# Operand sums of a seven-product scheme made on VectorE behind plain units, and gate weights given the highest priority

## The chip, the cores and the metric

The kernel runs on one core of a Trainium2 chip. The metric is device time of one execution in microseconds (us). The engines have the profile's names: PE is TensorE, PEld its weight loads, ACT is ScalarE, DVE is VectorE, POOL is GpSimd, SP is SyncE, which issues the transfers.

## The reference

A diffusion backbone of two layers (DEPTH 2, D_MODEL 1024) over 256 context and 512 latent tokens, in fp32. Each layer has an adaLN-modulated RMSNorm, one input projection, three mixers (mLSTM, attention, gated DeltaNet), a gated sum and an output projection, and then the part of this case: a second norm and a gated MLP with a width-3 convolution over the tokens.

```python
def dwconv(u, w):
    ...
    up = jnp.pad(u, ((0, 0), (p, p), (0, 0)))
    out = up[:, 0:t] * w[0]
    for j in range(1, k):
        out = out + up[:, j:j + t] * w[j]
    return out
```

The MLP has D_FF = 2816 value and as many gate columns: each is a product of the normed tokens with `w_up`, a convolution, then value times silu(gate), then a product with `w_down`. The scans (mLSTM and DeltaNet) get their gates from 16 + 16 columns of `w_in`.

## The kernel before

Every fp32 product is made of three matmuls on operands split into a high part h (rounded to the type that PE takes, by ACT) and a low part l = x - h (by DVE): h.xh, h.xl and l.xh. The token operand of the MLP is `n01xh`, `n01xl` (tile names have the layer as their second character; 768 tokens in layer 0, 512 in layer 1).

`ffn` walks D_FF in groups f0 = 0, 4, .. 20 of four 128-column blocks, each as two pairs p0 = 0, 2. A pair is a gate unit (`f0g<f0><p0>`, 256 columns) and a value unit (`f0a<f0><p0>`). The down product of a group (`f0d0`, ...) comes between the gate and value units of the next. There are two kinds of unit. A plain unit (`gemm_fm`, and `gemm_first` for the first) has two blocks of 48 matmuls: 24 over 512 tokens, 24 over 256. A unit of seven products (`gemm7`) cuts columns, rows and tokens in halves and does seven products in place of eight: 84 matmuls over 384 tokens. It needs sums of weights (`s23`, `s4`; four 128x512 additions on POOL, L321, for each unit) and sums of the token operand, T1 to T4, each with a high part and a low part (`n01Th`, `n01Tl`; T2 overwrites a quarter of xh and xl). `norm_sums` makes those once, in layer 0 alone. In layer 0 before, pair 0 is plain, and the other ten pairs (20 units) use seven products. In layer 1 all units are plain.

Behind each block the conv takes the PSUM result: one ACT activation, and two DVE steps (511 or 255 wide) that read PSUM. In the value unit follow the product with the gate (POOL, in place on f0a), a cast (ACT, f0gh) and a subtraction (DVE, f0gl). Between the units PE does small blocks for later adaLN weights (`adp`, `adc`, fed by loads `ad`).

The Tile framework writes the order of each engine's instructions ahead of time, from a simulated timeline and from priorities; `self.high(n)` raises (or, if negative, lowers) the priority of what it encloses, and weight loads and splits have it raised by `self.prio`. On the chip each engine goes through its list in order. `gates_mm` loads the gate columns of `w_in` in three pieces (`g0raw`, `g1raw`), splits them (`g0w`, `g1w`) and multiplies.

Of the kernel before, what the change touches and what calls it, by code (L numbers as in the profile page):

```python
# [20 lines left out]
NT = SEQ + CTX  # L21
# [9 lines left out]
A_Q, A_K, A_V, A_O, A_G = 0, 256, 512, 1024, 1536  # L31
# [74 lines left out]
class Kernel:  # L106
# [201 lines left out]
    def gemm7(self, src, c0, x, nt, done, nm):  # L308
# [313 lines left out]
    def norm_sums(self):  # L622


        nc, N = self.nc, self.N
        nm, n = N["nm"], N["nt"] // 2
        xh, xl = N["x"]
        q = lambda v, k, t: v[:, 4 * k:4 * k + 4, n * t:n * t + n]
        R = {}
        for k, t in ((0, 0), (0, 1), (1, 1), (1, 0)):  # L630
            R[k, t] = self.q6(f"{nm}R{k}{t}").rearrange("p (k t) -> p k t", k=4)
            nc.gpsimd.tensor_tensor(out=R[k, t], in0=q(xh, k, t).bitcast(F32), in1=q(xl, k, t).bitcast(F32), op=ALU.add)

        def sub(o, a, b):
            nc.vector.tensor_tensor(out=R[o], in0=R[a], in1=R[b], op=ALU.subtract)
        sub((0, 0), (0, 1), (0, 0))
        sub((0, 1), (1, 1), (0, 1))
        sub((1, 1), (1, 1), (0, 0))
        sub((1, 0), (1, 0), (1, 1))
        T = {}  # L640
        for i, o in ((3, (1, 1)), (1, (0, 0)), (4, (1, 0)), (2, (0, 1))):
            if i == 2:
                T[i] = q(xh, 0, 1), q(xl, 0, 1)
            else:
                T[i] = [self.q6(f"{nm}T{v}{i}", F32R).rearrange("p (k t) -> p k t", k=4) for v in "hl"]
            self.split(*T[i], R[o])
        return xh, xl, T

    def norm_sq(self, j, a, b, eng=None):
        nc, N = self.nc, self.N  # L650
# [125 lines left out]
    def gates_mm(self, l, xs, gc):  # L776

        nc = self.nc
        nm = f"g{l}"
        W = self.I["w_in"][l]  # L780
        n = 288
        h, lo = [self.gw(f"{nm}w{u}", u).rearrange("p (k c) -> p k c", k=KD) for u in range(2)]
        for k0 in (0, 3, 6):
            nk = min(3, KD - k0)
            raw = self.T([128, 1024], f"{nm}raw{k0}", tag="wraw", bufs=4)[:, :nk * n].rearrange("p (k c) -> p k c", k=nk)
            rows = W[128 * k0:128 * (k0 + nk), :].rearrange("(k p) c -> p k c", p=128)
            for o, c0, m in ((0, A_G, 16), (16, C_G, 16), (32, B_Q + 512, 256)):
                nc.sync.dma_start(raw[:, :, o:o + m], rows[:, :, c0:c0 + m])
            self.split(h[:, k0:k0 + nk], lo[:, k0:k0 + nk], raw)
        self.bp = self.dr.tile([6, 128, 768], F32, name=f"bp{l}", tag=f"bp{l}")  # L790

        banks = ((self.pb, self.pb, self.pl), (self.pl, self.pc, self.pb)) if l else ((self.pl, self.pl, self.pc),) * 2
        for r in range(2):
            pss = [p(f"{nm}ps{r}_{i}")[:, 0:n] for i, p in enumerate(banks[r])]
            for i, ps in enumerate(pss):
                tt = 3 * r + i
                (a, _), xh, xl = xs[tt // 4]
                t = slice(128 * tt - a, 128 * tt - a + 128)
                for k in range(KD):
# [994 lines left out]
    def ffn(self, l, xs, nt):  # L1794
# [6 lines left out]
        for f0 in range(0, NFF, FG):  # L1801
            fn = min(FG, NFF - f0)
            gh, gl = [], []
            for p0 in range(0, fn, 2):
# [36 lines left out]
                if down and f0 + FG < NFF:  # L1841
                    self.gemm_fm(*down)
                    down = None
                if x7:
                    self.gemm7(U, 128 * (f0 + p0), x7, nt, done_a, f"{nm}a{f0}{p0}")
                else:
                    self.gemm_fm(U, 128 * (f0 + p0), 256, KD, xs, done_a, f"{nm}a{f0}{p0}")
                    if f0 + p0 == 0 and nt == NT:
                        x7 = self.norm_sums()
            segs = [((a, b), Blocks(gh, a, b), Blocks(gl, a, b)) for a, b in segb]  # L1850

            def done_d(j, res):
# [73 lines left out]
    def body(self):  # L1926
# [5 lines left out]
        for l in range(DEPTH):  # L1932
# [9 lines left out]
            with tc.tile_pool(name=f"t{l + 1}", bufs=1, reuse_waits="tile") as self.ph:  # L1942
# [95 lines left out]
```

## Time and profile before

| | |
|---|---|
| median of 3 runs | 2674.77 us (2668.91 to 2679.19) |
| profiled execution, its own time | 2679.46 us |
| span of its profile, mean granted clock of PE | 2677.7 us, 0.987 |
| busy: PE, PEld, DVE, ACT, POOL | 97%, 83%, 63%, 39%, 17% |

The busy shares are of the span. With PE at 97%, time can only come from stretches in which PE stands still or runs at a lower granted clock, or from fewer or shorter matmuls. The profile shows where those stretches are, and which engine PE waits for in each.

### The profile page before, as it was taken

Reading aid. Unit: us, or ns where it says so; the run is one execution under the profiler, and the core shown is the slowest. Engines: PE = TensorE matmul, PEld = TensorE weight load, DVE = VectorE, ACT = ScalarE, POOL = GpSimd, SP = SyncE. Lnnn points to the kernel's source line nnn. Section 1 sums busy time; section 2 is a strip of 40 time slices with the busy share of each in tenths; the row PEclk is TensorE's granted clock in tenths of the full one; section 3 lists DMA queues with packets and bytes.
Section 4 is the critical chain, followed back from the end, with each engine's and each line's share of the span. In section 5 each row is a group of like instructions: output and inputs, shape, how many; then the busy total and the mean of one; then the engine's idle time right before and its main releaser. Section 6 shows DMA issues by size and latency. Waiting matters only on the chain.

```text
span 2677.7 us, 44644 instructions
## 1 busy us (share of the span) xinstructions
PE 2584.4 (97%) x17161; PEld 2234.9 (83%) x17161; DVE 1699.3 (63%) x3605; ACT 1047.1 (39%) x2313; POOL 463.1 (17%) x362
## 2 busy tenths in 40 slices
PE   7999999999999997999999999999999999999999
PEld 5987988888888886899999988888877878888887
DVE  6666566746534658676786777856676646655555
ACT  5433355333432234343443454344633333433332
POOL 1010000001110426154445320000000203100000
PEclk9999999999999998999999999999999999999999
DMA  8364343546746322322212243522367675333332
GB/s 284 94 178 134 90 121 88 151 137 195 214 160 230 120 87 87 107 83 79 71 54 81 87 141 102 154 71 77 114 193 219 184 249 150 91 94 95 95 103 75
DMA packets 485223, 344.19 MB, mean 129 GB/s; under 512 B 48168, under 2 KB 450322, under 8 KB 484242
## 3 DMA queue, kind: packets, MB, share of 16 engines
q1 hardware_dynamic: 484721, 338.19, 42.6%
q8 instruction: 135, 2.21, 0.3%
q10 hardware_dynamic: 288, 3.15, 0.3%
q14 instruction: 79, 0.64, 0.1%
HBM read 285.23 MB, written 56.03 MB: 127 GB/s over the span
## 4 chain that ended last, share of the span: by engine, by line
PE 75%; DVE 10%; DMA 9%; issue 2%; ACT 1%; POOL 1%; SPq 1%; DVEq 0%; POOLq 0%; ACTq 0%
PE mg04p L265 1%; PE mg04p L266 1%; PE mg04p L264 1%; PE y0p L265 1%; PE y0p L264 1%; PE y0p L266 1%; PE adp L541 1%; PE mg14p L264 1%; PE mg14p L265 1%; PE mg14p L266 1%; PE y1p L264 1%; DMA m1mb<-g1rd 1%; PE y0op L264 1%; PE y0op L266 1%; PE y0op L265 1%
## 5 line engine op out<-in xcount | busy, mean ns | idle before, releaser
L1830 POOL TENSOR_TENSOR f1a<-f1a,f1g 128x512 f32<-128x512 f32 x22 | 28.5, 1295 | 311.8 <-DVE f1a L1815 292.3
L541 PE MATMUL adp<-ad,s 128*32 128x256 f32 x640 | 55.7, 405 | 6.5 <-DMA ad<-ada_w 5.6
L1830 POOL TENSOR_TENSOR f0a<-f0a,f0g 128x768 f32<-128x768 f32 x22 | 51.9, 2360 | 57.8 <-DVE f0a L1815 53.4
L1752 POOL TENSOR_TENSOR y0a<-y0a,y0g 128x768 f32<-128x768 f32 x16 | 33.2, 2079 | 118.1 <-DVE y0g L1749 115.8
L1107 POOL TENSOR_TENSOR m0qz<-m0qz,m0e 64x512 f32<-64x512 f32 x12 | 15.5, 1295 | 165.5 <-DVE mg04s5l L225 68.7
L541 PEld LDWEIGHTS adp<-ad,s 128*32 128x32 f32 x640 | 18.5, 112 | 26.3 <-issue 14.2
L1832 DVE TENSOR_TENSOR f0gl<-f0a,f0gh 128x768 fp32r<-128x768 f32 x22 | 31.0, 1411 | 8.5 <-ACT f0gh L1831 8.5
L1752 POOL TENSOR_TENSOR y1a<-y1a,y1g 128x512 f32<-128x512 f32 x16 | 24.2, 1513 | 57.8 <-DVE y1g L1749 56.6
L544 ACT COPY adr<-adp 128x256 f32<-128x256 f32 x40 | 14.8, 370 | 44.0 <-PE adp L541 42.8
L1831 ACT CAST f0gh<-f0a 128x768 fp32r<-128x768 f32 x22 | 18.4, 838 | 33.5 <-POOL f0a L1830 33.5
L1013 ACT ACTIVATE mg0t<-mg04p 128x512 f32<-128x512 f32 (+1 forms) x40 | 19.5, 486 | 25.2 <-PE mg04p L266 20.7
L1107 POOL TENSOR_TENSOR m1qz<-m1qz,m1e 64x512 f32<-64x512 f32 x8 | 11.2, 1406 | 102.9 <-DMA m1mb<-g1rd 45.7
L1821 ACT ACTIVATE f0g<-f0g 128x768 f32<-128x768 f32 x22 | 18.5, 846 | 22.8 <-DVE f0g L1815 22.8
L1749 DVE SCALAR_TENSOR_TENSOR y0g<-y0g,y0p 128x512 f32<-128x512 f32 (+1 forms) x32 | 17.3, 549 | 15.8 <-PE y0p L266 14.0
L1821 ACT ACTIVATE f1g<-f1g 128x512 f32<-128x512 f32 x22 | 13.9, 630 | 32.5 <-DVE f1g L1815 32.5
L1096 DVE SCALAR_TENSOR_TENSOR m0mb<-m0mb,g0a,cst 128x128 f32<-128x128 f32 x48 | 16.6, 404 | 15.3 <-DMA m0mb<-g0rd 14.3
L1773 DVE SCALAR_TENSOR_TENSOR hr<-y0op,y0gh,hr 128x512 f32<-128x512 f32 (+1 forms) x16 | 9.9, 617 | 25.8 <-PE y0op L266 25.8
L1169 POOL TENSOR_TENSOR rt<-rc,rw 128x256 f32<-128x256 f32 x4 | 3.0, 745 | 115.7 <-PE b0pk L1239 54.8
L1832 DVE TENSOR_TENSOR f1gl<-f1a,f1gh 128x512 fp32r<-128x512 f32 x22 | 15.1, 685 | 10.9 <-ACT f1gh L1831 10.7
L1831 ACT CAST f1gh<-f1a 128x512 fp32r<-128x512 f32 x22 | 13.5, 616 | 16.6 <-POOL f1a L1830 16.6
L1729 DVE TENSOR_TENSOR y0l<-y0ld,y0h 128x768 fp32r<-128x768 f32 x12 | 12.8, 1091 | 11.3 <-ACT y0h L1728 11.3
L1098 ACT ACTIVATE m0mb<-m0mb 128x512 f32<-128x512 f32 x12 | 7.6, 631 | 30.1 <-DVE m0mb L1096 25.4
(4586 smaller groups left out, 10220.2 us busy)
## 6 DMA issues: line engine op xcount, KB each, us to landing
ad<-ada_w SPq DMA_DIRECT2D x96, 512.0 KB, 4.3
mg04r<-w_in SPq DMA_DIRECT2D x20, 512.0 KB, 5.1
mg14r<-w_in SPq DMA_DIRECT2D x20, 512.0 KB, 6.0
y0g<-mg SPq DMA_DIRECT2D x24, 384.0 KB, 4.4
mg<-mg0t SPq DMA_DIRECT2D x24, 256.0 KB, 3.1
y0r<-w_branch SPq DMA_DIRECT2D x12, 512.0 KB, 3.6
mg<-mg1t SPq DMA_DIRECT2D x24, 256.0 KB, 3.5
y1r<-w_branch SPq DMA_DIRECT2D x12, 512.0 KB, 3.9
```

Source lines behind the costliest of these rows:

```text
L264: nc.tensor.matmul(o, hv[:, k, :], xh[:, k, :], start=(k == 0), stop=False)
L265: nc.tensor.matmul(o, hv[:, k, :], xl[:, k, :], start=False, stop=False)
L266: nc.tensor.matmul(o, lv[:, k, :], xh[:, k, :], start=False, stop=(k == nk - 1))
L541: nc.tensor.matmul(ps[32 * j:32 * j + 32, 0:256], self.s32[:, 2 * k:2 * k + 32], raw[:, j, :], start=(q == 0), stop=(q == 1), tile_positio ...
L1013: nc.scalar.activation(s, o, AF.Tanh, scale=0.5)
L1107: nc.gpsimd.tensor_tensor(out=qd[r, d], in0=qd[r, d], in1=e2[r], op=ALU.mult)
L1749: nc.vector.scalar_tensor_tensor(out=(a if i == BR[0] else gt)[:, s:e], in0=gt[:, s:e], scalar=1.0, in1=ps, op0=ALU.add, op1=ALU.mult)
L1752: nc.gpsimd.tensor_tensor(out=a[:, :nt], in0=a[:, :nt], in1=gt[:, :nt], op=ALU.add)
L1821: nc.scalar.activation(a[:, :nt], a[:, :nt], AF.Silu)
L1830: nc.gpsimd.tensor_tensor(out=a[:, :nt], in0=a[:, :nt], in1=keep[b][:, :nt], op=ALU.mult)
L1831: nc.scalar.copy(h, a[:, :nt])
L1832: nc.vector.tensor_tensor(out=gl[-1][:, b, :nt], in0=a[:, :nt], in1=h.bitcast(F32), op=ALU.subtract)
```

## The change

Pairs 0 and 2 of group 0 are plain now, and the seven products begin with pair 4, 18 units in place of 20. `norm_sums` is called ahead of the value unit of pair 2, at a priority lowered by 3000. It makes no sums on POOL: ten instructions of 128x1536 on DVE and four splits, in two buffers R in place of four. The split of T2, which overwrites xh and xl, is made by `last_sum()` behind the plain unit. The buffer s4 is single, and the pool of q6 tiles has 11 in place of 10. In `gates_mm` of both layers the loads and splits have their priority raised by 100000.

```diff
@@ -313,7 +313,7 @@
         xh, xl, T = x
         r0, r1 = [self.wraw(src[:, c0 + 128 * b:c0 + 128 * b + 128], KD, 128, f"{nm}r{b}") for b in range(2)]
         s23 = self.pi.tile([128, KD, 128], F32, name=f"{nm}s23", tag="s23", bufs=2)
-        s4 = self.pi.tile([128, 4, 128], F32, name=f"{nm}s4", tag="s4", bufs=2)
+        s4 = self.pi.tile([128, 4, 128], F32, name=f"{nm}s4", tag="s4", bufs=1)
         lo, hi = slice(0, 4), slice(4, 8)
 
         def half(out, a, b, op):
@@ -626,25 +626,37 @@
         nm, n = N["nm"], N["nt"] // 2
         xh, xl = N["x"]
         q = lambda v, k, t: v[:, 4 * k:4 * k + 4, n * t:n * t + n]
-        R = {}
-        for k, t in ((0, 0), (0, 1), (1, 1), (1, 0)):
-            R[k, t] = self.q6(f"{nm}R{k}{t}").rearrange("p (k t) -> p k t", k=4)
-            nc.gpsimd.tensor_tensor(out=R[k, t], in0=q(xh, k, t).bitcast(F32), in1=q(xl, k, t).bitcast(F32), op=ALU.add)
-
-        def sub(o, a, b):
-            nc.vector.tensor_tensor(out=R[o], in0=R[a], in1=R[b], op=ALU.subtract)
-        sub((0, 0), (0, 1), (0, 0))
-        sub((0, 1), (1, 1), (0, 1))
-        sub((1, 1), (1, 1), (0, 0))
-        sub((1, 0), (1, 0), (1, 1))
+        R = [self.q6(f"{nm}R{i}").rearrange("p (k t) -> p k t", k=4) for i in range(2)]
         T = {}
-        for i, o in ((3, (1, 1)), (1, (0, 0)), (4, (1, 0)), (2, (0, 1))):
-            if i == 2:
-                T[i] = q(xh, 0, 1), q(xl, 0, 1)
-            else:
-                T[i] = [self.q6(f"{nm}T{v}{i}", F32R).rearrange("p (k t) -> p k t", k=4) for v in "hl"]
-            self.split(*T[i], R[o])
-        return xh, xl, T
+
+        def op(o, a, b, op):
+            nc.vector.tensor_tensor(out=o, in0=a, in1=b, op=op)
+
+        def diff(i, j, k):
+
+            for o, v in zip(R, (xh, xl)):
+                op(o, q(v, *j).bitcast(F32), q(v, *k).bitcast(F32), ALU.subtract)
+            op(R[0], R[0], R[1], ALU.add)
+
+        def less(o, j, a):
+            op(o, q(xh, *j).bitcast(F32), a, ALU.subtract)
+            op(o, o, q(xl, *j).bitcast(F32), ALU.add)
+
+        def split(i, v):
+            T[i] = [self.q6(f"{nm}T{p}{i}", F32R).rearrange("p (k t) -> p k t", k=4) for p in "hl"]
+            self.split(*T[i], v)
+        diff(1, (0, 1), (0, 0))
+        split(1, R[0])
+        less(R[1], (1, 1), R[0])
+        split(3, R[1])
+        less(R[0], (1, 0), R[1])
+        split(4, R[0])
+        diff(2, (1, 1), (0, 1))
+        T[2] = q(xh, 0, 1), q(xl, 0, 1)
+
+        def last():
+            self.split(*T[2], R[0])
+        return (xh, xl, T), last
 
     def norm_sq(self, j, a, b, eng=None):
         nc, N = self.nc, self.N
@@ -784,9 +796,10 @@
             nk = min(3, KD - k0)
             raw = self.T([128, 1024], f"{nm}raw{k0}", tag="wraw", bufs=4)[:, :nk * n].rearrange("p (k c) -> p k c", k=nk)
             rows = W[128 * k0:128 * (k0 + nk), :].rearrange("(k p) c -> p k c", p=128)
-            for o, c0, m in ((0, A_G, 16), (16, C_G, 16), (32, B_Q + 512, 256)):
-                nc.sync.dma_start(raw[:, :, o:o + m], rows[:, :, c0:c0 + m])
-            self.split(h[:, k0:k0 + nk], lo[:, k0:k0 + nk], raw)
+            with self.high(100000):
+                for o, c0, m in ((0, A_G, 16), (16, C_G, 16), (32, B_Q + 512, 256)):
+                    nc.sync.dma_start(raw[:, :, o:o + m], rows[:, :, c0:c0 + m])
+                self.split(h[:, k0:k0 + nk], lo[:, k0:k0 + nk], raw)
         self.bp = self.dr.tile([6, 128, 768], F32, name=f"bp{l}", tag=f"bp{l}")
 
         banks = ((self.pb, self.pb, self.pl), (self.pl, self.pc, self.pb)) if l else ((self.pl, self.pl, self.pc),) * 2
@@ -1841,12 +1854,16 @@
                 if down and f0 + FG < NFF:
                     self.gemm_fm(*down)
                     down = None
+                if f0 + p0 == 2 and nt == NT:
+                    with self.high(-3000):
+                        sums, last_sum = self.norm_sums()
                 if x7:
                     self.gemm7(U, 128 * (f0 + p0), x7, nt, done_a, f"{nm}a{f0}{p0}")
                 else:
                     self.gemm_fm(U, 128 * (f0 + p0), 256, KD, xs, done_a, f"{nm}a{f0}{p0}")
-                    if f0 + p0 == 0 and nt == NT:
-                        x7 = self.norm_sums()
+                    if f0 + p0 == 2 and nt == NT:
+                        x7 = sums
+                        last_sum()
             segs = [((a, b), Blocks(gh, a, b), Blocks(gl, a, b)) for a, b in segb]
 
             def done_d(j, res):
@@ -1950,7 +1967,7 @@
                 else:
                     self.ada_fill(2)
                 self.spare = nt < NT
-                with self.inner(f"u{l}", 10):
+                with self.inner(f"u{l}", 11):
                     xs = self.ffn(l, xs, nt)
                 self.dump_h(f"hf{l}", nt)
                 if l + 1 < DEPTH:
```

DVE, behind the plain unit f0a00 of layer 0 (n01R, n01T are the sums, f0a and f0g conv steps, ada for later weights). Before:

```order
L635 TENSOR_TENSOR n01R_11192<-n01R_11194,n01R_11192 128x1536
L574 TENSOR_REDUCE ada_103<-adc_3_11517 128x4
L580 TENSOR_TENSOR ada_103<-ada_103,vec 128x16
L635 TENSOR_TENSOR n01R_11194<-n01R_11196,n01R_11194 128x1536
L574 TENSOR_REDUCE ada_103<-adc_4_11679 128x4
L635 TENSOR_TENSOR n01R_11196<-n01R_11196,n01R_11192 128x1536
L225 TENSOR_TENSOR n01xl<-n01R_11194,n01xh 128x4x384
L635 TENSOR_TENSOR n01R_11198<-n01R_11198,n01R_11196 128x1536
L225 TENSOR_TENSOR n01Tl_11205<-n01R_11196,n01Th_11204 128x1536
L1832 TENSOR_TENSOR f0gl_11107<-f0a_11182,f0gh_11106 128x768
L225 TENSOR_TENSOR n01Tl_11209<-n01R_11192,n01Th_11208 128x1536
```

After, at the same place; f0a02s0l is the low part of a plain weight:

```order
L633 TENSOR_TENSOR n01R_11339<-n01xh 128x1536
L633 TENSOR_TENSOR n01R_11340<-n01xl 128x1536
L1826 SCALAR_TENSOR_TENSOR f0a_11182<-f0a00p_0_11132,vec,f0a_11182 128x511
L225 TENSOR_TENSOR f0a02s0l<-f0a02r_11363,f0a02s0h 128x1024
L633 TENSOR_TENSOR n01R_11339<-n01R_11339,n01R_11340 128x1536
L1826 SCALAR_TENSOR_TENSOR f0a_11182<-f0a00p_512_11157,vec,f0a_11182 128x255
L1828 SCALAR_TENSOR_TENSOR f0a_11182<-f0a00p_0_11132,vec,f0a_11182 128x511
L633 TENSOR_TENSOR n01R_11340<-n01xh,n01R_11339 128x1536
L1828 SCALAR_TENSOR_TENSOR f0a_11182<-f0a00p_512_11157,vec,f0a_11182 128x255
L225 TENSOR_TENSOR n01Tl_11345<-n01R_11339,n01Th_11344 128x1536
L1826 SCALAR_TENSOR_TENSOR f0g_11248<-f0g02p_0_11198,vec,f0g_11248 128x511
L633 TENSOR_TENSOR n01R_11340<-n01R_11340,n01xl 128x1536
```

The sums stand between the conv steps and weight splits, ten additions or subtractions in place of four; the last split, of n01xl, comes 39 rows further on, here with its neighbours:

```order
L633 TENSOR_TENSOR n01R_11339<-n01xh 128x1536
L1828 SCALAR_TENSOR_TENSOR f0a_11419<-f0a02p_0_11369,vec,f0a_11419 128x511
L580 TENSOR_TENSOR ada_103<-ada_103,vec 128x16
L1828 SCALAR_TENSOR_TENSOR f0a_11419<-f0a02p_512_11394,vec,f0a_11419 128x255
L633 TENSOR_TENSOR n01R_11339<-n01R_11339,n01R_11340 128x1536
L1826 SCALAR_TENSOR_TENSOR f0a_11507<-f0a02p_0_11457,vec,f0a_11507 128x511
L1828 SCALAR_TENSOR_TENSOR f0a_11507<-f0a02p_0_11457,vec,f0a_11507 128x511
L225 TENSOR_TENSOR n01xl<-n01R_11339,n01xh 128x4x384
L1845 TENSOR_TENSOR f0gl_11427<-f0a_11419,f0gh_11426 128x768
L225 TENSOR_TENSOR f0g40w1l<-f0g40r_11521,f0g40w1h 128x1024
```

It is followed by the low part of the third weight of `f0g40`, the first unit of seven products now.

POOL at the same place (L1830, after L1843, is value times gate; L321 the weight sums; L632 the sums of the operand). Before:

```order
L1830 TENSOR_TENSOR f0a_11099<-f0a_11099,f0g_11027 128x768
L321 TENSOR_TENSOR f0g02s_11223<-f0g02r_11218,f0g02s_11222 128x512
L632 TENSOR_TENSOR n01R_11192<-n01xh,n01xl 128x1536
L632 TENSOR_TENSOR n01R_11194<-n01xh,n01xl 128x1536
L632 TENSOR_TENSOR n01R_11196<-n01xh,n01xl 128x1536
L632 TENSOR_TENSOR n01R_11198<-n01xh,n01xl 128x1536
L1830 TENSOR_TENSOR f0a_11182<-f0a_11182,f0g_11035 128x768
L321 TENSOR_TENSOR f0a02s_11381<-f0a02r_11377,f0a02r_11379 128x512
L225 TENSOR_TENSOR f0g02w4l<-f0g02s_11223,f0g02w4h 128x512
L321 TENSOR_TENSOR f0g40s_11547<-f0g40r_11543,f0g40r_11545 128x512
L321 TENSOR_TENSOR f0a02r_11379<-f0a02r_11379 128x512
```

After:

```order
L1843 TENSOR_TENSOR f0a_11099<-f0a_11099,f0g_11027 128x768
L1843 TENSOR_TENSOR f0a_11182<-f0a_11182,f0g_11035 128x768
L321 TENSOR_TENSOR f0g40s_11523<-f0g40r_11519,f0g40r_11521 128x512
L321 TENSOR_TENSOR f0g40r_11521<-f0g40r_11521 128x512
L321 TENSOR_TENSOR f0g40s_11523<-f0g40r_11521,f0g40r_11519 128x512
L321 TENSOR_TENSOR f0g40s_11524<-f0g40r_11519,f0g40s_11523 128x512
L1843 TENSOR_TENSOR f0a_11419<-f0a_11419,f0g_11248 128x768
L1843 TENSOR_TENSOR f0a_11507<-f0a_11507,f0g_11331 128x768
```

The four additions of 128x1536 and the weight sums of the units `f0g02` and `f0a02` are gone.

ACT at the start of layer 1 (g1w are the gate weights, c10k0a and c10k0t conv and silu of the first key block, c10qs1h a weight). Before:

```order
L1365 ACTIVATE c10k0a_16193<-c10kp_0_16045,vec 128x512
L224 CAST g1w_16267<-g1raw_16269 128x864
L224 CAST g1w_16267<-g1raw_16275 128x864
L224 CAST g1w_16267<-g1raw_16281 128x576
L1371 ACTIVATE c10k0t_16197<-c10k0a_16193 128x512
L224 CAST c10qs1h<-c10qr_16623 128x1024
L1365 ACTIVATE c10k0a_16200<-c10kp_1_16047,vec 128x256
```

After:

```order
L224 CAST g1w_16243<-g1raw_16245 128x864
L224 CAST g1w_16243<-g1raw_16251 128x864
L224 CAST g1w_16243<-g1raw_16257 128x576
L1378 ACTIVATE c10k0a_16169<-c10kp_0_16021,vec 128x512
L224 CAST c10qs1h<-c10qr_16599 128x1024
L1384 ACTIVATE c10k0t_16173<-c10k0a_16169 128x512
L1378 ACTIVATE c10k0a_16176<-c10kp_1_16023,vec 128x256
```

The three casts stand ahead of the conv step, and the weight cast c10qs1h ahead of the silu c10k0t.

## Rows read from the trace of the kernel before

**Rows 1.** The page, busy time of the engines

```profile
PE 2584.4 (97%) x17161; PEld 2234.9 (83%) x17161; DVE 1699.3 (63%) x3605; ACT 1047.1 (39%) x2313; POOL 463.1 (17%) x362
```

**Rows 2.** Window of the stretch, core 0, busy us of each engine

```profile
1034.15:1094.89 60.74, 42.47 (x225) 35.84 (x224) 50.42 (x41) 20.73 (x27) 42.72 (x15) 0.78 0.29 87
```

**Rows 3.** Waits of PE, 1015 to 1100 us: total, times, longest

```profile
PE adp L541 <- DMA ad<-ada_w: 5.6, 2, 5.4
...
PE f0g02x L334 <- ACT n01xh L224: 4.4, 1, 4.4
...
PE f0g02x L334 <- ACT n01Th L224: 2.6, 1, 2.6
```

**Rows 4.** Timeline of POOL: start, us, instruction

```profile
1029.32 1.85 POOL L1830 TENSOR_TENSOR f0a<-f0a,f0g 128x768 f32<-128x768 f32 x1
...
1033.37 16.88 POOL L632 TENSOR_TENSOR n01R<-n01xh,n01xl 128x1536 f32<-128x1536 f32 x4
...
1050.21 3.41 POOL L1830 TENSOR_TENSOR f0a<-f0a,f0g 128x768 f32<-128x768 f32 x1
...
1059.10 2.81 POOL L321 TENSOR_TENSOR f0g40s<-f0g40r,f0g40r 128x512 f32<-128x512 f32 x1
...
1074.29 1.27 POOL L321 TENSOR_TENSOR f0g40s<-f0g40r,f0g40s 128x512 f32<-128x512 f32 x1
```

**Rows 5.** Timeline of DVE: start, us, instruction

```profile
1021.78 1.21 DVE L225 TENSOR_TENSOR f0g02w0l<-f0g02r,f0g02w0h 128x1024 fp32r<-128x1024 f32 x1
...
1022.91 0.47 DVE L1813 SCALAR_TENSOR_TENSOR f0a<-f0a00p,vec,f0a 128x255 f32<-128x255 f32 x1
...
1034.92 0.75 DVE L1815 SCALAR_TENSOR_TENSOR f0a<-f0a00p,vec,f0a 128x511 f32<-128x511 f32 x1
...
1050.21 1.74 DVE L635 TENSOR_TENSOR n01R<-n01R,n01R 128x1536 f32<-128x1536 f32 x1
...
1051.98 3.25 DVE L635 TENSOR_TENSOR n01R<-n01R,n01R 128x1536 f32<-128x1536 f32 x1
...
1057.90 2.85 DVE L635 TENSOR_TENSOR n01R<-n01R,n01R 128x1536 f32<-128x1536 f32 x1
```

**Rows 6.** Timeline of PE: start, us, instruction

```profile
1034.15 0.34 PE L334 MATMUL f0g02x<-n01xh,f0g02w0h 128*128 128x384 f32 x1
...
1094.89 0.34 PE L334 MATMUL f0g40x<-n01xh,f0g40w0h 128*128 128x384 f32 x1
...
1131.59 0.39 PE L264 MATMUL f0d0p<-f0gh,f0d0s4h 128*128 128x512 f32 x1
...
1134.34 0.28 PE L264 MATMUL f0d0p<-f0gh,f0d0s4h 128*128 128x256 f32 x1
...
1135.75 0.38 PE L573 MATMUL adc<-cst,adr 128*128 128x128 f32 x2
...
1137.06 0.50 PE L264 MATMUL f0d0p<-f0gh,f0d0s5h 128*128 128x512 f32 x1
```

**Rows 7.** Window of one unit of seven products, its instructions alone

```profile
1175.00:1200.00 25.00, 15.07 (x84) 14.61 (x84) 2.75 (x5) 0.93 (x2) 1.00 0.11 32
```

**Rows 8.** The page, costliest groups: busy and mean ns

```profile
L1832 DVE TENSOR_TENSOR f0gl<-f0a,f0gh 128x768 fp32r<-128x768 f32 x22 | 31.0, 1411 | 8.5 <-ACT f0gh L1831 8.5
```

**Rows 9.** DMA issues of 1033 to 1060 us: KB, us to landing

```profile
f0g40r<-w_up SPq DMA_DIRECT2D x2, 512.0 KB, 5.2
```

**Rows 10.** Windows of 2 us behind the waits, all engines

```profile
1074.00:1076.00 2.00, 2.00 (x9) 1.99 (x8) 0.31 (x1) 0.00 (x0) 1.56 (x2) 0.54 0.26 61
...
1076.00:1078.00 2.00, 2.00 (x9) 2.00 (x8) 0.00 (x0) 0.00 (x0) 0.00 (x0) 0.60 0.61 200
```

**Rows 11.** Waits of PE, 1575 to 1600 us

```profile
PE g1ps L802 <- DVE g1w L225: 3.0, 1, 3.0
```

**Rows 12.** Timeline of ScalarE (ACT) at the start of layer 1

```profile
1578.00 2.29 ACT L224 CAST g1w<-g1raw 128x864 fp32r<-128x864 f32 x3
```

**Rows 13.** Waits of PE, 1100 to 1200 us

```profile
PE f0g42x L334 <- POOL f0g42w4l L225: 0.2, 1, 0.2
```

## Prediction

> **What bounds the kernel now.** I read the page first: TensorE (PE) is busy 97% of the span [rows 1], so only a stretch where it is not busy can give time back without removing products. The slices of the page show one such stretch behind the head, about 1,030 to 1,095 us. Its window [rows 2] shows PE busy for 42.47 of 60.74 us, at a mean granted clock of 0.78: it idles, and part of its work runs at the lower of its two levels. The waits of PE there [rows 3] name the cause: `f0g02x`, the first unit with seven products, waits for the operand sums `n01xh`, `n01Th` (only the largest rows are shown), and the ada weights and the next unit's split queue behind. The timeline of GpSimd (POOL) [rows 4] has the four additions that begin the sums: 16.88 us, from 1033.37 to 1050.2, begun just when the plain unit `f0a00` ends. VectorE (DVE) then subtracts and splits beside POOL's weight sums; there a 128x1536 subtraction takes 2.85 us (beside `f0g40s`) or 3.25 us (beside the f0a multiply), alone 1.74 us [rows 5].
>
> **What the change costs and moves.** The place is the time from the start of `f0g02` at 1034.15 to the start of `f0g40` at 1094.89, 60.74 us [rows 6].
>
> Plain units in place of two of seven products. From the down products of group 0 [rows 6]: twelve 512-column matmuls take 1134.34 - 1131.59 = 2.75 us, twelve of 256 columns 1135.75 - 1134.34 = 1.41 us. A plain unit has 48 of each: 4 x 4.16 = 16.64 us. A unit of seven products is 84 matmuls, 15.07 us busy [rows 7]. So the two units cost 2 x 1.57 = 3.1 us more work. One ada block (16 + 2 small matmuls) is 1137.06 - 1135.75 = 1.31 us [rows 6].
>
> The new stretch without waits: 1034.15 + 2 x 16.64 + 2 x 1.31 = 1070.0 is where `f0g40` could start, 24.9 us sooner. The order has one more ada block behind that point than before, so 1.3 us goes back: **23.6 us** at most from this place.
>
> What VectorE must do meanwhile. POOL gives up the four additions, and the weight sums of two units (no row of them stands in the order after). The f0a multiply that came at 1029.32 [rows 4] no longer has three weight sums ahead, so I let the sums start at 1031.7 on DVE. From there to the end of `n01xl` the order of the changed kernel has, on DVE: 14 of 128x1536 (10 sums, 4 splits) at 1.74 = 24.4; ten 511-wide conv steps at 0.75 = 7.5; eight 255-wide at 0.47 = 3.8; four weight splits at 1.21 = 4.8; one f0gl at 1.41; 0.5 for tiny ones: 42.4 us [rows 5, 8]. Uncontended, T2's low part is ready at 1074.1. `f0g40` needs it after 12 + 12 matmuls (4.3 us, at a seventh of 15.07 us for 12), an ada block, and a few matmuls on T2's high part (0.5 us, my estimate): about 1070.0 + 4.3 + 1.3 + 0.5 = 1076.1. So DVE has 2.0 us to spare; the conv steps that release PSUM banks between the sums have margins of the same size.
>
> What takes the margin. POOL still does one f0a multiply and the four weight sums of `f0g40` beside that chain (its second raw tile is issued once `f0a02s1l` has been read, about 1052.8 by the same walk, and lands some 5.2 us later [rows 9]). By the pairs in [rows 4, 5] the multiply costs DVE 3.25 - 1.74 = 1.51 us, each weight sum 2.85 - 1.74 = 1.11: 5.95 us together. DVE is late by 5.95 - 2.0 = 4.0 us, and PE waits that long at the start of `f0g40`, in one or several pieces. After the waits near 1071 to 1074 the clock was 0.54 and 0.60 over 4 us [rows 10], which gave away 2 x 0.46 + 2 x 0.40 = 1.7 us; I take it once. Residual: 5.7 us. Bounds: 0 (all hidden), and 14 x 1.11 - 2.0 = 13.5 us with 3.4 of clock, 16.9 us, if POOL met every one of the 14. I stay with 5.7, as POOL's list there has five instructions.
>
> The Trainium skill (SBUF — State Buffer, "SBUF: two separate sides") says that a VectorE instruction with two SBUF operands and a GpSimd instruction exclude one another for the whole instruction. Its sum would be POOL's own times, 1.85 + 4 x 1.27 = 6.9 us in place of 5.95, so 1 us less gain; the rows lie near it (1.74 + 1.27 = 3.01 against 2.85 and 2.81), and the sum goes by the rows.
>
> Gate weights first. In layer 1 PE waits 3.0 us for `g1w` [rows 11]. The order after moves only the three casts on ScalarE, 2.29 us [rows 12], ahead of `c10k0a`; on DVE the low parts still stand behind the conv steps, which now start later by up to 2.3 us, partly taken up by the wait for `c10qs1h`. I reckon 1 us lost there. In layer 0 the same three casts move ahead of `c00k0a`, and `c00k0t` is no longer behind them: some 0.7 us gained. The g0raw loads pass ad_3_3 and ad_1_0 to ad_1_2 on SP's queue, six issues earlier; the PE work on these waits for earlier adaLN work anyway. Net 0, bounds -3 and +3 (the wait gone, or doubled).
>
> One s4 buffer in place of two. The fourth weight sum of a unit now stands behind the w4 split of the unit before on POOL. PE waits for a w4 split only 0.2 us in such a place [rows 13]. Cover: the unit is 15 us long and the sum 1.27. I take 0; without cover it costs 1.27 us for each of 18 calls, 23 us. The order of layer 1's mixers also shifts (some 480 rows of PE, the same instructions): 0, bounds -3 and +3.
>
> **Sum.** 23.6 - 5.7 = 17.9 us off the profiled execution's 2679.46: 2661.6. That execution is 4.7 us above the median of 2674.77, so the predicted median is **2657**. A measurement here can tell about 0.5%, 13.4 us, from no change.
>
> **Rivals.** (A) The forecast, partly hidden: 2657, chance 0.48, own range 2650 to 2662. (B) All hidden: POOL's five instructions fall beside conv steps that read PSUM, which were not stretched (0.75 us at 1034.92, during POOL's additions [rows 4, 5]). Then 23.6: **2651**, chance 0.17. Against it: the DVE list has no gap to fall into. (C) DVE much later: the upper bound of 16.9 us, 2674.8 - 6.7 = **2668**; PE then waits at each PSUM bank and at T3, T2 and T1 in turn. For it: any idle time of DVE in its list, a cast on ScalarE that comes late, counts in full once the 2.0 us are gone; and 24.4 of its 42.4 us are open to contention. Chance 0.27. (D) Nothing to see, 2671 to 2678: the conv steps of `f0g02` and `f0a02` queue behind sums, and the stall of before only moves; it would need 20 us of new waits. Chance 0.04. (E) Slower: the single s4 buffer. If POOL, in its order, holds the f0a multiply behind a fourth sum that waits for the w4 split of a unit not yet reached by PE, every seven-product unit shows a wait. The price must pass 17.9 + 13.4 = 31.3 us, 1.7 us for each of 18 calls, against 1.27 us for the sum alone; at 2.5 us each the time is 2657 + 45 = **2702**. Against it: those units wait 0.2 us now. Chance 0.04.
>
> The skill's rule, read as a result of its own, gives 2658 and falls in (A).
>
> **How the numbers follow.** Leaving 1 in 10 on either side: below, (B) and a better split of layer 1, 2648; above, the larger part of (C), 2669. Faster by over 0.5% means below 2661.4: most of (A), all of (B) and a little of (C), 0.66. Slower: 0.04. Same: 0.30.
>
> **What would show it.** Right: POOL has no 128x1536 additions; `f0g40` begins near 1070 to 1076; the window from 1034 has PE above 0.9 busy and the clock near 1; PE's remaining wait there names `n01xh`, `n01xl` or `f0g40w23l`, 3 to 6 us in all; the wait for `g1w` is still about 3 to 4 us. Wrong: waits of PE for conv steps inside `f0g02` or `f0a02`, a 128x1536 instruction of DVE above 2.2 us on average, new waits for w4 splits in units 4 to 20, or more than 3 us lost in the mixers of layer 1.

## The result and the profile after

The changed kernel takes 2659.69 us (median of 5 runs, 2656.56 to 2661.14) against 2674.77 us: ratio 0.9934, 95% interval 0.9919 to 0.9948. Timed again beside other kernels (e9 below) the ratio was 0.9914, 0.9901 to 0.9928, so 18 to 23 us are gained by the ratios, which are not the quotients of the medians but lie within 0.001 of them; the two medians themselves differ by 15.1 us. Forecast were 17.9 us, and a median of 2657 where 2659.69 came.

The page of the kernel after, busy times; it answers to [rows 1]:

```profile
PE 2586.3 (97%) x17185; PEld 2235.7 (84%) x17185; DVE 1689.9 (64%) x3599; ACT 1042.6 (39%) x2305; POOL 420.8 (16%) x348
```

The stretch from the start of `f0g02` (1040.86 now; the window is cut at 1040.90) to the start of `f0g40` (1078.20), by the windows of the changed kernel (span, then busy us of PE, PEld, DVE, ACT and POOL, granted clock, DMA share, GB/s), and all of PE's waits from 1035 to 1095; they answer to [rows 2, 3, 6]:

```profile
1040.90:1078.20 37.30, 36.71 (x230) 30.70 (x229) 36.16 (x37) 15.34 (x20) 12.46 (x5) 1.00 0.32 97
```

```profile
PE f0g40x L334 <- DVE ada L580: 0.6, 1, 0.6
```

60.74 us have become 37.30, PE is busy for 36.71 of them, and the clock stays at 1.00. A single wait of 0.6 us is left. The stall is not shortened: it is gone, 23.4 us.

DVE and POOL of the kernel after in that stretch (start, us, instruction); they answer to [rows 4, 5]:

```profile
1040.89 1.75 DVE L633 TENSOR_TENSOR n01R<-n01xh 128x1536 f32<-128x1536 f32 x1
...
1053.13 2.74 DVE L633 TENSOR_TENSOR n01R<-n01R,n01xl 128x1536 f32<-128x1536 f32 x1
...
1066.51 2.45 DVE L633 TENSOR_TENSOR n01R<-n01xl 128x1536 f32<-128x1536 f32 x1
...
1069.54 2.18 DVE L225 TENSOR_TENSOR n01Tl<-n01R,n01Th 128x1536 fp32r<-128x1536 f32 x1
...
1074.00 1.34 DVE L225 TENSOR_TENSOR f0g40w23l<-f0g40s,f0g40w23h 128x1024 fp32r<-128x1024 f32 x1 [1.14 <-ACT f0g40w23h L224]
...
1081.80 1.76 DVE L225 TENSOR_TENSOR n01xl<-n01R,n01xh 128x1536 fp32r<-128x1536 f32 x1 [0.15 <-ACT n01xh L224]
```

```profile
1033.84 1.84 POOL L1843 TENSOR_TENSOR f0a<-f0a,f0g 128x768 f32<-128x768 f32 x1 [29.84 <-DVE f0a L1828]
1051.03 3.23 POOL L1843 TENSOR_TENSOR f0a<-f0a,f0g 128x768 f32<-128x768 f32 x1 [15.35 <-DVE f0a L1828]
1064.80 2.55 POOL L321 TENSOR_TENSOR f0g40s<-f0g40r,f0g40r 128x512 f32<-128x512 f32 x1 [10.54 <-DMA f0g40r<-w_up]
1067.43 2.68 POOL L321 TENSOR_TENSOR f0g40r<-f0g40r 128x512 f32<-128x512 f32 x1
1070.18 2.70 POOL L321 TENSOR_TENSOR f0g40s<-f0g40r,f0g40r 128x512 f32<-128x512 f32 x1
1072.96 1.30 POOL L321 TENSOR_TENSOR f0g40s<-f0g40r,f0g40s 128x512 f32<-128x512 f32 x1
1078.68 3.24 POOL L1843 TENSOR_TENSOR f0a<-f0a,f0g 128x768 f32<-128x768 f32 x1 [4.42 <-DVE f0a L1828]
```

DVE's list runs from 1040.89 to 1081.80 + 1.76 = 1083.56, 42.7 us. Where POOL works beside it, the instruction of POOL is stretched (2.55 to 2.70 for a weight sum that takes 1.30 at 1072.96, 3.23 and 3.24 for a multiply that takes 1.84 at 1033.84), by 6.8 us in all. Of DVE's sums and splits only three are (2.74, 2.45, 2.18, against 1.74 or 1.75), by 2.1 us. PE at the start of `f0g40`:

```profile
1078.20 0.42 PE L334 MATMUL f0g40x<-n01xh,f0g40w0h 128*128 128x384 f32 x1 [0.60 <-DVE ada L580]
...
1082.45 0.38 PE L573 MATMUL adc<-cst,adr 128*128 128x128 f32 x2
...
1083.68 1.06 PE L541 MATMUL adp<-ad,s 128*32 128x256 f32 x14
...
1084.96 0.34 PE L334 MATMUL f0g40x<-n01xl,f0g40w23h 128*128 128x384 f32 x1
```

`n01xl`, the last split, is ready at 1083.56, and the first matmul that reads it starts at 1084.96: 1.4 us are to spare.

### The profile page after: what moved, and what is told of

Its sections match the earlier page's. It is cut to its first block, busy times and chain, and to the rows that moved or that the text cites. A ratio compares the mean times of both kernels' runs of the same rounds, so it can differ in the third digit from the quotient of the medians.

```text
span 2657.9 us, 44659 instructions
## 1 busy us (share of the span) xinstructions
PE 2586.3 (97%) x17185; PEld 2235.7 (84%) x17185; DVE 1689.9 (64%) x3599; ACT 1042.6 (39%) x2305; POOL 420.8 (16%) x348
## 3 DMA queue, kind: packets, MB, share of 16 engines
q1 hardware_dynamic: 484721, 338.19, 42.7%
## 4 chain that ended last, share of the span: by engine, by line
PE 80%; DVE 8%; DMA 6%; issue 2%; ACT 1%; SPq 1%; POOL 1%; DVEq 0%; ACTq 0%; POOLq 0%
PE mg04p L265 2%; PE mg04p L266 2%; PE mg04p L264 2%; PE adp L541 1%; PE y0p L264 1%; PE y0p L265 1%; PE y0p L266 1%; PE mg14p L264 1%; PE mg14p L266 1%; PE mg14p L265 1%; PE y1p L264 1%; PE y1p L265 1%; PE y1p L266 1%; DMA ad<-ada_w 1%; PE y0op L265 1%
## 5 line engine op out<-in xcount | busy, mean ns | idle before, releaser
L1843 POOL TENSOR_TENSOR f1a<-f1a,f1g 128x512 f32<-128x512 f32 x22 | 28.5, 1295 | 312.1 <-DVE f1a L1828 292.6
L1843 POOL TENSOR_TENSOR f0a<-f0a,f0g 128x768 f32<-128x768 f32 x22 | 52.5, 2389 | 95.6 <-DVE f0a L1828 95.6
L1120 POOL TENSOR_TENSOR m0qz<-m0qz,m0e 64x512 f32<-64x512 f32 x12 | 16.6, 1383 | 166.5 <-DVE b0a3P L1338 69.4
L1845 DVE TENSOR_TENSOR f1gl<-f1a,f1gh 128x512 fp32r<-128x512 f32 x22 | 15.1, 685 | 10.9 <-ACT f1gh L1844 10.7
L1844 ACT CAST f1gh<-f1a 128x512 fp32r<-128x512 f32 x22 | 13.5, 616 | 16.6 <-POOL f1a L1843 16.6
```

Of the source, the lines that this page charges most:

```text
L1120: nc.gpsimd.tensor_tensor(out=qd[r, d], in0=qd[r, d], in1=e2[r], op=ALU.mult)
L1843: nc.gpsimd.tensor_tensor(out=a[:, :nt], in0=a[:, :nt], in1=keep[b][:, :nt], op=ALU.mult)
L1844: nc.scalar.copy(h, a[:, :nt])
L1845: nc.vector.tensor_tensor(out=gl[-1][:, b, :nt], in0=a[:, :nt], in1=h.bitcast(F32), op=ALU.subtract)
```

## The experiments

Theory 1: the gain is made in that stretch, because plain products hide the sums. Rival: it is the engine (GpSimd's additions) that counted. For the rest of the span the question is which of the smaller differences between the two profiles belong to the change, and which to the execution. Each kernel's ratio is to the kernel before, on the same chip (before: 2679.6 us for e1 to e4, 2679.43 for e5 to e8, 2680.83 for e9 to e12).

**e1, the raised priority alone.** The kernel before with

```diff
-            for o, c0, m in ((0, A_G, 16), (16, C_G, 16), (32, B_Q + 512, 256)):
+            with self.high(100000):
+                for o, c0, m in ((0, A_G, 16), (16, C_G, 16), (32, B_Q + 512, 256)):
...
```

> The kernel before with the raised priority of the gate weights alone; sums, units and s4 as before. Theory 1 (all of the gain is in the stretch from f0g02 to f0g40): the time is that of before, ratio 0.999 to 1.001; the 3.0 us wait for g1w in layer 1 becomes a wait of about 3.3 us for c10kq, and the 6 us by which layer 1's mixers are shorter in the profile after do not show again, since they are run-to-run variation. Rival theory (the changed order of layer 1's mixers, which comes with the gate priority, is worth 6 us and the changed head costs 3): 2671 to 2672 us, the mixers of layer 1 shorter by 5 to 7 us and the head longer by about 3 in its profile.

2675.79 us, ratio 0.9986 (0.9976 to 0.9995), faster by 0.14%, 3.8 us. The interval reaches theory 1's 0.999 to 1.001 as well as the rival's figure (as a ratio 0.9986 to 0.999), so the time alone does not decide. The profile speaks for the rival: layer 1's mixers took 663.3 us for 673.8, and the head was 3 us longer. The wait in layer 1 moved as expected (c10kq 2.9, g1w 0.7).

**e2, the change without the raised priority.**

```diff
-            with self.high(100000):
-                for o, c0, m in ((0, A_G, 16), (16, C_G, 16), (32, B_Q + 512, 256)):
...
+            for o, c0, m in ((0, A_G, 16), (16, C_G, 16), (32, B_Q + 512, 256)):
```

> The changed kernel without the raised priority of the gate weights. Theory 1: the whole gain stands here, 2657 to 2662 us, f0g40 begins 44 us after f0a00 ends (60.7 before) and PE waits under 1 us in between. Rival theory (the mixers of layer 1 gain by the gate priority): 3 us slower than the changed kernel, 2662 to 2665 us, and the mixers of layer 1 as long as before.

2666.07 us, 0.9951 (0.9939 to 0.9963), 13.1 us less than before by the ratio. The stretch takes 37.6 us and PE waits 0.9 us in it, so the mechanism there is theory 1's. (The 44 us expected are a difference between two traces, 1078.20 - 1034.15; the kernel after has 37.3.) Whether the whole gain stands here the time leaves open: as ratios, theory 1 gave 0.9934 to 0.9952 and the rival 0.9952 to 0.9964. The profile speaks for the rival, as the mixers of layer 1 took 681.3 us.

**e3, one s4 buffer alone.** The kernel before with

```diff
-        s4 = self.pi.tile([128, 4, 128], F32, name=f"{nm}s4", tag="s4", bufs=2)
+        s4 = self.pi.tile([128, 4, 128], F32, name=f"{nm}s4", tag="s4", bufs=1)
```

> The kernel before with one s4 buffer in place of two; only the order of GpSimd changes. In the profile after, the time from f0g40 to f0g200 is 2.1 us longer than before, and f0a162 waits 2.2 us for its w4 split. Theory 1 (the single buffer costs this): 2676 to 2677 us, the same wait at f0a162x, the time from f0g40 to f0g200 longer by 1.5 to 2.5 us. Rival (variation of the run, or the sums' new place): no wait for a w4 split above 0.5 us, 2674 to 2675 us.

2681.89 us, 1.0014 (1.0004 to 1.0024), slower by 0.14%, 3.8 us (2.3 us by the medians). Its profile has the wait of the kernel after; PE's waits of e3, 1440 to 1500 us:

```profile
PE f0a162x L334 <- POOL f0a162w4l L225: 2.1, 1, 2.1
```

f0a162 to f0g200 takes 18.1 us in place of 16.6; from f0g40 to f0g200 it is only 0.7 us more, less than expected. POOL and SP of the kernel after show the way there:

```profile
1446.59 2.01 POOL L321 TENSOR_TENSOR f0a162s<-f0a162r,f0a162s 128x512 f32<-128x512 f32 x1
1454.82 1.30 POOL L321 TENSOR_TENSOR f0a200s<-f0a200r,f0a200r 128x512 f32<-128x512 f32 x1 [6.22 <-DMA f0a200r<-w_up]
...
1457.45 2.25 POOL L225 TENSOR_TENSOR f0a162w4l<-f0a162s,f0a162w4h 128x512 fp32r<-128x512 f32 x1
...
1448.63 1.45 SPq L233 DMA_DIRECT2D f0a200r<-w_up  x2
```

f0a162's fourth weight sum now comes late in POOL's list (1446.59) and ends at 1448.60. It reads a raw weight tile, and SP issues the next unit's load, f0a200r, at 1448.63, 0.03 us later. Those data land at 1454.8; POOL's list has two sums of f0a200 ahead of f0a162's w4 split, for which PE waits 2.2 us.

**e4, sums on VectorE with one plain pair.**

```diff
-                if f0 + p0 == 2 and nt == NT:
+                if f0 + p0 == 0 and nt == NT:
...
-                    if f0 + p0 == 2 and nt == NT:
+                    if f0 + p0 == 0 and nt == NT:
```

> The changed kernel with one plain pair in place of two: the sums are all made on VectorE, but beside f0a00, and seven products begin with f0g02 as before. Theory 1 (the cover by 36 us of plain products is what hides the sums; VectorE alone needs 44 us for its list): PE still waits some 20 us at f0g02, 2664 to 2672 us. Rival theory (taking GpSimd's 17 us out is what counts, wherever the sums stand): under 2661 us, since two units fewer are plain, and under 8 us of waits at f0g02 and f0a02.

2682.2 us, 1.0003 (0.9991 to 1.0015): nothing gained, slower than both theories had it (as ratios 0.996 to 0.999, and under 0.9949). PE's waits of e4, 990 to 1095 us:

```profile
PE f0g02x L334 <- ACT n01xh L224: 9.8, 1, 9.8
PE adp L541 <- DMA ad<-ada_w: 2.0, 1, 2.0
...
PE f0g02x L334 <- DVE n01xl L225: 1.9, 1, 1.9
```

The stretch from f0g02 to f0g40 takes 54.3 us, 6.4 less than before. The waits of f0g02 in it are 13.4 us, where theory 1 had some 20 and the rival under 8. The stretch ahead of it (f0g00 to f0g02) takes 43.7 for 40.9, the head is 1.8 us longer, f0a162 1.6 and layer 1's mixers 3.8, so nothing is left. Without the second plain pair most of the stall stays, though VectorE makes the sums: the rival falls.

**e5, sums as before at the new place.** Four additions on GpSimd, four subtractions and four splits on VectorE, called where the change calls them (a tile pool has another name there, too):

```diff
-        R = [self.q6(f"{nm}R{i}").rearrange("p (k t) -> p k t", k=4) for i in range(2)]
...
+        R = {}
+        for k, t in ((0, 0), (0, 1), (1, 1), (1, 0)):
+            R[k, t] = self.q6(f"{nm}R{k}{t}").rearrange("p (k t) -> p k t", k=4)
+            nc.gpsimd.tensor_tensor(out=R[k, t], in0=q(xh, k, t).bitcast(F32), in1=q(xl, k, t).bitcast(F32), op=ALU.add)
```

> The changed kernel with the sums as before (four additions on GpSimd, four subtractions and four splits on VectorE) but at the new place, beside the plain units f0g02 and f0a02. Theory 1 (the cover of 36 us of plain products is what counts): as fast as the changed kernel within 3 us, ratio to before 0.992 to 0.9955, PE waits under 2 us from f0g02 to f0g80. Rival theory (the engine counts, GpSimd and VectorE stretch each other's instructions): over 5 us slower than the changed kernel, ratio 0.9955 to 0.999, with waits for n01xh or n01Th at the start of f0g40.

2663.03 us, 0.9939 (0.9926 to 0.9951). This is theory 1's range, but beside the changed kernel's two ratios (0.9934 and 0.9914) it is 1 or 7 us slower, so the time alone leaves the rival's 5 us open. The waits decide: those for n01xh or n01Th that the rival asked for do not occur, and the stretch takes 41.6 us, 4.3 more than with VectorE's sums and 19.1 less than before. Theory 1 again, with one wait over its 2 us; PE's wait there, and POOL and DVE beside it in e5:

```profile
PE f0a02p L264 <- DVE f0g L1820: 3.6, 1, 3.6
```

```profile
1031.84 16.58 POOL L632 TENSOR_TENSOR n01R<-n01xh,n01xl 128x1536 f32<-128x1536 f32 x4
...
1036.36 4.26 DVE L1837 TENSOR_TENSOR f0gl<-f0a,f0gh 128x768 fp32r<-128x768 f32 x1
...
1045.91 4.13 DVE L635 TENSOR_TENSOR n01R<-n01R,n01R 128x1536 f32<-128x1536 f32 x1
```

GpSimd's 16.58 us stretch VectorE's instructions to 4.26 and 4.13 us (0.95 and 1.74 in the kernel after), a conv step comes late, and PE waits 3.6 us for its PSUM bank at f0a02. That is what VectorE saves here: 3.6 us of wait, 4.3 of the stretch, of some 23.

**e6, nine more instructions on VectorE.** The changed kernel with the three that make the last sum run four times, which changes no result:

```diff
-        diff(2, (1, 1), (0, 1))
+        for _ in range(4):
+            diff(2, (1, 1), (0, 1))
```

> The changed kernel with the three instructions that make the last sum run four times, nine more of 128x1536 on VectorE, 15.7 us at 1.74. In the changed kernel n01xl is ready at 1083.56 and first read at 1084.96. Theory 1 (the cover is all but used up, 1.4 us are left): PE waits 13 to 16 us at the start of f0g40, mostly for n01xh, n01xl or PSUM banks, and the time from the start of f0g02 to that of f0g80 grows by 14 to 18 us. Rival (much of VectorE's list could wait, so that there is more cover than that one gap shows): under 8 us.

2673.11 us, one run. The windows of the changed kernel and of e6 from the start of f0g02 to that of f0g80:

```profile
1040.90:1180.90 140.00, 138.01 (x850) 122.38 (x849) 104.44 (x134) 54.51 (x79) 53.00 (x29) 1.00 0.36 106
```

```profile
1037.00:1193.50 156.50, 141.68 (x851) 123.09 (x850) 120.53 (x143) 54.14 (x80) 55.88 (x29) 0.96 0.32 95
```

156.50 - 140.00 = 16.5 us for 15.7 us of added work less 1.4 of margin; DVE's busy time there grew by 16.1, and the clock fell to 0.96. PE's two largest waits of e6, 1030 to 1200 us, and the first product that reads `n01xl`:

```profile
PE adp L541 <- DMA ad<-ada_w: 7.5, 3, 3.6
PE f0g40x L334 <- DVE n01xl L225: 1.5, 1, 1.5
```

```profile
1102.74 0.69 PE L334 MATMUL f0g40x<-n01xl,f0g40w23h 128*128 128x384 f32 x1 [1.49 <-DVE n01xl L225]
```

Theory 1 holds for the size: the cover is all but used up, and PE ends up waiting for `n01xl`. It does not hold for the names of the waits. Only 2.4 us are for `n01xl` and `n01xh`; 7.5 us are for loads of ada weights, as the order of e6 has three ada blocks ahead of the products that read T2, where the changed kernel has one.

**e7 and e10, two s4 buffers.** The changed kernel, the same for both labels, with

```diff
-        s4 = self.pi.tile([128, 4, 128], F32, name=f"{nm}s4", tag="s4", bufs=1)
+        s4 = self.pi.tile([128, 4, 128], F32, name=f"{nm}s4", tag="s4", bufs=2)
...
-                with self.inner(f"u{l}", 11):
+                with self.inner(f"u{l}", 10):
```

> The changed kernel with two s4 buffers and ten q6 tiles in place of one and eleven; the order of layer 1's mixers is the same. Theory 1 (the single buffer costs 1.5 us at f0a162 and up to 3.6 us in all): 1.5 to 3.6 us faster than the changed kernel, ratio to before 0.992 to 0.9928, no wait for a w4 split above 0.5 us. Rival (ten q6 tiles hold up the f0gl of pair 2 and with it f0d0): 0 to 3 us slower, with a wait at f0d0p.

> The kernel with two s4 buffers and ten q6 tiles again. Its profile showed 1.9 us less from f0g40 to f0g200 than the changed kernel, its median 9 us less by ratio. Theory 1 (only what the profile shows by place is real, the rest is variation between executions): 1 to 4 us faster than the changed kernel of this call. Rival (the whole 9 us belong to the change): 7 to 11 us faster.

e7: 2651.48 us, 0.9899 (0.9884 to 0.9914). e10, the same program: 2656.31 us, 0.9912 (0.9898 to 0.9925), against 2658.0 us for the changed kernel beside it, 1.7 us faster. So theory 1: the wait for a w4 split at f0a162 is gone in both profiles (16.7 us from f0a162 to f0g200), and the 9 us of e7 were mostly between chips and executions. The single medians bound the 1.7 no better than some 3 us.

**e8, the raised priority in layer 1 alone.** (Its label says two s4; it has one, as the changed kernel.)

```diff
-            with self.high(100000):
+            with self.high(100000 * l):
```

> The changed kernel with the raised priority in layer 1 alone (s4 single as in the changed kernel). The head has the order of before, layer 1's mixers nearly that of the changed kernel. Theory 1 (the head loses 2 to 3 us by the casts that stand ahead of c00k0a): 2 to 3 us faster than the changed kernel, ratio 0.992 to 0.9928, the value products of layer 0 (c00vp) begin at 101 to 102 us in place of 104.4. Rival (the head differs by the run alone): as the changed kernel, c00vp at 103 to 105 us.

2655.96 us, 0.991 (0.9897 to 0.9924), faster than theory 1's 0.992 to 0.9928; beside the changed kernel's two ratios the gain is 1 or 6 us. `c00vp` begins at 99.4, even earlier than expected.

**e9, e11 and e12, beside e10 on one chip.** e9 is the changed kernel, e11 has e8's edit and e7's, e12 has e7's edit and no raised priority at all.

> The changed kernel itself, timed beside the next three on one chip, so that differences of a few us are not read across chips. Both theories: ratio 0.992 to 0.9948, the interval of its first measurement.

> Raised priority of the gate weights in layer 1 alone, two s4 buffers and ten q6 tiles, all else as in the changed kernel. Theory 1 (head 2.9 us, s4 1.9 us, layer 1's mixers as in the changed kernel): 4 to 7 us faster than the changed kernel of this call. Rival (the single results of the two edits add up, 9 and 6 us): 12 to 16 us faster.

> No raised priority in either layer, two s4 buffers and ten q6 tiles, sums as in the changed kernel. The head has the order of before (2.9 us gained on the changed kernel), s4 1.9 us gained, layer 1's mixers nearly the order of before. Theory (that order costs 6 to 10 us): 1 to 5 us slower than the changed kernel of this call. Rival (the order of the mixers costs nothing, the profiles differ by variation): 4 to 6 us faster than the changed kernel, as the kernel with layer 1's gates raised.

e9: 2658.0 us, 0.9914 (0.9901 to 0.9928). e11: 2655.61 us, 0.9905 (0.989 to 0.992), 2.4 us faster than e9 where 4 to 7 were expected; the intervals of e9, e10 and e11 overlap, so which is fastest is open. The rival (12 to 16) falls. e12: 2662.2 us, 0.9931 (0.9919 to 0.9944), 4.2 us slower than e9, as the theory has it. e11 and e12 differ by the raised priority in layer 1 alone: 6.6 us, and none of their executions overlap (2652.30 to 2656.21 against 2658.59 to 2664.79).

**All profiles by place.** The times between the first matmuls of a few tiles, one profile each, in us, from starts read to 0.1 us: the start of `c00vp` (head), f0g02 to f0g40, f0a162 to f0g200, `c10vp` to `f1g00p` (layer 1's mixers to the end of its gated sum), and `m0S` to `y0p` (mLSTM of layer 0, whose order on every engine is the same in all kernels).

| kernel | head | f0g02 to f0g40 | f0a162 to f0g200 | layer 1 mixers | m0S to y0p |
|---|---|---|---|---|---|
| before | 101.4 | 60.7 | 16.6 | 673.8 | 210.6 |
| changed | 104.4 | 37.3 | 18.1 | 667.8 | 213.4 |
| e1 | 104.7 | 60.8 | 16.7 | 663.3 | 209.7 |
| e2 | 101.1 | 37.6 | 18.0 | 681.3 | 210.2 |
| e3 | 102.1 | 60.7 | 18.1 | 674.9 | 215.3 |
| e4 | 103.2 | 54.3 | 18.3 | 677.6 | 209.9 |
| e5 | 103.4 | 41.6 | 18.6 | 668.2 | 212.9 |
| e6 | 104.2 | 38.0 | 18.2 | 669.3 | 209.1 |
| e7 | 103.7 | 38.0 | 16.7 | 664.3 | 209.2 |
| e8 | 99.4 | 37.9 | 18.6 | 670.3 | 210.6 |
| e9 | 103.5 | 36.8 | 18.2 | 667.1 | 210.0 |
| e10 | 105.2 | 38.5 | 16.7 | 666.8 | 211.0 |
| e11 | 101.7 | 36.8 | 16.7 | 672.0 | 211.4 |
| e12 | 101.3 | 36.5 | 16.6 | 681.7 | 211.4 |

Head: with the raised priority in layer 0 (eight profiles) 103.2 to 105.2, mean 104.0; without (six) 99.4 to 102.1, mean 101.2. s4: one buffer 18.0 to 18.6, two 16.6 or 16.7. Mixers: with the order of the changed kernel or one near it (by their lists of instructions) 663.3 to 672.0 (nine profiles), with that of before or one near it 673.8 to 681.7 (before, e2, e3, e4, e12). e4 tells the priority from the order: it has the raised priority, and its casts of `g1w` stand ahead of the conv step, but the scheduler gave its PE nearly the order of before in the mixers, and it has the time of before.

## Why the prediction was right in the sum, and in which steps it was not

The forecast of 2657 and the sign hold. The steps stand differently, and errors of both signs cancel.

1. **The stall and its cause** held. 60.74 us became 37.30; the forecast without waits was 1070.0 - 1034.15 = 35.9. The two plain units and their ada blocks took 0.8 us longer, and there is the wait of 0.6. Of the 24.9 us up to the start of `f0g40` 23.4 came, and the ada block that was to go back behind that point is there: five blocks between f0g40 and f0g200, four in the kernel before.

2. **The residual wait of 5.7 us** did not come: 0.6 us, under another name (`ada`), and no lower clock. This is the term that was mis-sized, and for the stretch the time of rival (B) is what came. The step that failed is "What takes the margin". I took for each of POOL's five instructions (there were six, a second f0a multiply at 1078.68) the stretch that DVE had in [rows 5], 5.95 us. The trace after shows 1.0, 0.7 and 0.4 on three sums or splits, 2.1 us. Between VectorE's sums stand conv steps that read PSUM (0.47 to 0.75 us, not stretched), and POOL goes ahead there or is itself the one that waits: it lost 6.8 us. My own rows had that side, too: the 1.74 us that I called alone starts at 1050.21, together with POOL's multiply, which took 3.41 for the 1.85 of 1029.32 [rows 4, 5].

   The rule of the Trainium skill (SBUF — State Buffer, "SBUF: two separate sides") lets the one that starts first go on and the other wait. That agrees with the trace (1.30 alone, 2.55 to 2.70 beside VectorE), but my sum by it, POOL's whole 6.9 us laid on VectorE, was further off than the rows: here POOL did most of the waiting.

   The rest of the margin came out right by errors that cancel. Relative to the start of f0g02, VectorE began 2.4 us later than I let it, and PE reached the last split 2.1 us later. The list took 42.7 us, nearly the 42.4 of the sum without contention, though it had 2.1 us of stretch and 1.3 of idle time in it: adding up durations counts too much, as each instruction starts a little before the one ahead of it ends (1042.56 behind 1040.89 + 1.75), 2.8 us over the forty of the list. So that 1.4 us of margin were left is in part luck; e6 shows that so small a margin is real.

3. **The raised priority, "net 0"**: 0 was wrong by place. In layer 0 I had 0.7 us gained; it costs 2.8 (the means of the head). About half of that is there before the first gate cast. ACT's cast of a key weight, `c00ks1h`, starts 1.5 us later in the eight profiles with the raised priority in layer 0 than in the six without (means 47.2 and 45.7), and the norm behind it as well; in the kernels before and after it waits, by the profile, for a load of `g0raw`:

```profile
45.79 1.05 ACT L224 CAST c00ks1h<-c00kr 128x1024 fp32r<-128x1024 f32 x1 [0.32 <-DMA g0raw<-w_in]
```

```profile
47.60 1.05 ACT L224 CAST c00ks1h<-c00kr 128x1024 fp32r<-128x1024 f32 x1 [2.84 <-DMA g0raw<-w_in]
```

So the loads that pass others on SP's queue, which I had at no cost, have one; no run moves them without the casts. The other half comes at the casts. They do not only pass an activation: ACT stands still ahead of them (2.15 us, for which the profile names no releaser), and `c00k0a` behind them. ACT of the kernel after, and PE's wait at that place:

```profile
60.01 2.30 ACT L224 CAST g0w<-g0raw 128x864 fp32r<-128x864 f32 x3 [2.15 <-issue]
62.22 0.68 ACT L1378 ACTIVATE c00k0a<-c00kp,vec 128x512 f32<-128x512 f32 x1
```

```profile
64.61 0.37 PE L813 MATMUL g0ps<-g0w,n00xh 128*128 128x288 f32 x1 [2.22 <-DVE c00k0a L1381]
```

In the kernel before the same activation stood at 57.28, as soon as its product ended; the DVE steps behind it release a bank that PE needs. e8 takes the edit out in layer 0, and its head is as short as that of before. In layer 1 the wait for `g1w`, which I expected to stay at 3 to 4 us, fell to 0.7, and one for c10kq of 3.3 us came in its place; the start of layer 1 (c10kp to c10vp) is 0.6 us longer, where 1 was forecast.

4. **Layer 1's mixers, "0, bounds -3 and +3"**: 6 us less in the profile after, and by the means of the table 667.7 against 677.9, 10 us. The bound failed. It goes with the order that the scheduler made, not with the early weights (e4), and e11 against e12 shows it in the time, 6.6 us. Which of the moved rows bring it was not tried; among PE's waits there, those for m1hs (2.2), y1a (2.6) and c11r (2.3) of the kernel before are gone or under 1 us, and that for b1a3P grew from 2.6 to 4.0.

5. **One s4 buffer, "0"**: 1.6 us at f0a162 (the means of the table, 18.3 and 16.7), and 3.8 us by e3's ratio (2.3 by its medians), of which 1.5 are seen by place. A new wait for a w4 split was one of my signs of being wrong; it showed once, for 2.2 us. Rival (E), a wait in each of 18 calls, did not come: the cover that I named holds in all but one.

6. Against the forecast's 17.9 us, the profiles differ by 2677.7 - 2657.9 = 19.8: 23.4 in the stretch, 6.0 in layer 1's mixers, less 3.0 in the head, 2.1 from f0g40 to f0g200, 0.6 at the start of layer 1 and 3.6 in the mixers of layer 0, whose order is unchanged (2.8 of it in mLSTM). The residue is 0.3. Of the 2.1 us some 1.3 are the ada block that the forecast of 23.6 had already taken off, so the place itself gave 23.4 - 1.3 = 22.1 us, 4.2 more than the 17.9. These 4.2, and 6.0 in layer 1, were mostly paid back by the head, by s4, by the start of layer 1 and by the variation of layer 0's mixers. The mechanism at the place was right; that the whole came within 2 us of the forecast is luck.

## What to carry to other kernels

Ask first how many microseconds of other work lie between the operands' readiness and their first use: 36 us of plain products hid sums that cost 24 us of VectorE (e6: with little over 1 us to spare), and hid all but 4 us of them on GpSimd as well (e5), while VectorE without that cover took 6.4 us off the stretch, and nothing of it showed in the whole (e4). Where a priority is raised in a kernel whose order a scheduler makes, each stretch whose order changes has to be counted, also those far from the edit; here one such stretch brought more than the edit cost at its own place. Taking a buffer away can cost time at a second place: it makes an instruction late, and the other tile that this instruction reads is released late, too, and with it the next load into that tile (the kernel after and e3).

## What the runs showed that was not expected

With the same order on all engines, mLSTM of layer 0 took 209.1 to 215.3 us in the fourteen profiles (the last column), so a difference of 3 us between two single profiles is no sign of an edit there. And the same program stood at 0.9899 and 0.9912 (e7, e10), and at 0.9934 and 0.9914 (changed, e9): the second ratio of the changed kernel lies outside the interval of its first.
